# Other places in memory for the score tiles and the mask tiles, a VectorE add, unfilled gather tiles and another order of expert items

## The chip, the cores and the metric

One core of a Trainium2 chip runs the whole program. The metric is the time of one execution in microseconds (us); the kernel before has a median of 2927.58 us over 3 runs. Below, PE is TensorE, DVE is VectorE, ACT is ScalarE, POOL is GpSimd, and SP is the engine that issues most of the transfers.

## The reference

One decoder layer over T = 2048 tokens of D = 1024. The first half reads one projection of the normalised input and feeds three mixers: gated linear attention (GLA), attention over the 256 best keys of each query by an indexer score (DSA), and a complex diagonal state space (S5). The second half sends each token to 2 of 32 experts.

```
proj = h @ w_in                                  # 2616 columns, cut into GLA, DSA, indexer, S5 parts
score = einsum('bqh,bqhs->bqs', iwb, relu(iq . ik));  _, sel = top_k(score, 256)   # per block of 128 queries
p = softmax(q . k[sel]);  o_dsa = p @ v[sel]
x1 = x + gate1 * (concat([o_gla, o_dsa, o_s5]) @ w_out)
h2 = rms_norm(x1) * (1 + scale2) + shift2        # xn * g2r + s2r in the kernel
y  = sum over the 2 experts of  weight * (silu(h2 @ w_gate[e]) * (h2 @ w_up[e])) @ w_down[e]
out = rms_norm(x1 + gate2 * y)
```

## The kernel before, in words

Queries are worked in 16 blocks of 128. The parts that matter here follow each other.

**Scores** (to about 413 us). `ts`, `s1c` and `s1` are the pools of this stage. `s1c` and `s1` hold inputs and weights that are finished first, `ts` holds the rows `sb` in which the score of a block is summed on DVE (line 256) up to the end. Each block is stored to `score_d` (line 263).

**Sweeps, select and masks** (to about 756 us). Three pieces of one generator, `sweep2`, go over the tokens: token-major columns (32 rows `ot`, finished on DVE in line 209), the GLA queries and keys (no DVE finish, but DVE and POOL split their weights, line 467), and more token-major columns (16 rows `ot` of 128 elements for DVE). Their tiles lie in the pool `fp`. POOL issues the loads `xx` of the activations (line 440), SP those of the weights (`wstage`, line 175). Beside them runs `select`: the scores of blocks 2 to 15 come back into the tiles `scr` (line 509, 8.7 MB in all, pool `tks`), and ten iterations count the keys above a threshold, nine blocks on ACT (line 804), five on DVE (line 807), and move the threshold (lines 811 and on). `masks` then finds the exact threshold: per block the tile `pen` is written (line 857, DVE), the score is subtracted (line 858, POOL for blocks 2, 4, 6, 8, 10, else DVE), its eight largest are taken (line 859, DVE); some small operations follow (lines 865 to 882), and then for each block the mask `mk` is written (line 885) and stored. `pen` (two buffers) and `mk` are in the pool `pn`. `s5_tables(0)` is woven in (lines 931 to 959, DVE).

**A branch** on a check of the masks (tile `fi`) is read by all engines; GLA and S5, attention and output projection come behind it.

**Routing and experts** (from about 1580 us). In the output projection each block computes x1 (lines 1726, 1728) and xn, adds `s2r` and stores to `h2_d` (lines 1735 to 1737); `route` scatters token lists to `tab_d` (POOL, line 1440). A short chain of small operations on the counts of tokens then ranks the experts, and the loop takes 32 items in a fixed order, each with a fixed capacity from the list `CAP`, the expert of that rank being read at run time. Even items are the full ones, odd items the small ones. Each item gathers rows into the tiles `xg` and later `part` (POOL, lines 1877 and 2004, three buffers each, filled with zeros once in line 1832).

The program is written by a scheduler that fixes the order on each engine at build time from the waits it knows, memory among them: a tile may be written only when what lay in its place has been released, and the pools are placed as stacks on the two sides of memory.

Of the kernel before, what the change touches and what calls it, by code (L numbers as in the profile page):

```python
# [11 lines left out]
BF = mybir.dt.bfloat16  # L12
# [3 lines left out]
OP = mybir.AluOpType  # L16
# [4 lines left out]
P = 128  # L21
T = 2048
# [18 lines left out]
def body(tc, x, c, ada_w, ada_b, norm1_g, w_in, gla_gate_w, gla_gate_b, gla_norm_g, dsa_norm_g,  # L41
         s5_a_re, s5_a_im, s5_log_step, s5_b_re, s5_b_im, s5_c_re, s5_c_im, s5_d, s5_glu_w,
         s5_glu_b, s5_norm_g, w_out, norm2_g, router_grp_w, router_grp_b, router_exp_w,
         router_exp_b, exp_w_gate, exp_w_up, exp_w_down, final_norm_g, out, stop=None, dbg=None):
# [3 lines left out]
    V, S, G, TE = nc.vector, nc.scalar, nc.gpsimd, nc.tensor  # L48
# [175 lines left out]
    ssq = con.tile([P, NB], F32, name="ssq")  # L224

    p1x = ExitStack()
    ts_ = p1x.enter_context(tc.tile_pool(name="ts", bufs=1, side="right"))
    s1c = p1x.enter_context(tc.tile_pool(name="s1c", bufs=1, side="right"))
    s1 = p1x.enter_context(tc.tile_pool(name="s1", bufs=2, side="right"))
    s1p = p1x.enter_context(tc.tile_pool(name="s1p", bufs=1, space=PSUM, side="right"))  # L230
    pr = s1p.tile([P, 16], F32, name="pr", tag="pp", bufs=1, padded_shape=[P, C1])
    eps = ts_.tile([P, T], F32, name="eps")
# [177 lines left out]
    for ch in range(8):  # L410
        side = chain(tok1(ch), prep(ch + 1) if ch < 7 else ())
# [320 lines left out]
    NE, TW = 32, 8  # L732
    tab_d = dr.tile([NE * T, TW], F32, name="tab_d")
    h2_d = dr.tile([T + 1, D], F32, name="h2_d")
    yp_d = dr.tile([T + 1, D], F32, name="yp_d")
# [108 lines left out]
    def masks(blks, act, z, pn):  # L844
        lo, cl, cnt, up, dn, f, w = sels.pop(z)
        n_b, b0 = len(blks), blks[0]

        def tt(nm):
            return tk.tile([P, n_b], F32, name=nm, tag=f"tk{z}_{nm}", bufs=1)

        ntau, pv = tt("ntau"), tt("pv")
        tops = tk.tile([P, n_b, 8], F32, name=f"tops{z}")
        V.tensor_scalar(w, cl, -float(TOPK), None, op0=OP.add)
        for n, b in enumerate(blks):
            nk = (b + 1) * P
            pen = pn.tile([P, T], F32, name="pen")
            V.tensor_scalar(pen[:, :nk], scr[b], lo[:, n:n + 1], -4.0 * BIG, op0=OP.is_lt, op1=OP.mult)
            (G if b in GP else V).tensor_sub(pen[:, :nk], pen[:, :nk], scr[b])
            V.max(tops[:, n], pen[:, :nk])
            yield  # L860
        if act:

            wa, la = w[:, 0:act], lo[:, 0:act]
            for j, d in ((0, cnt), (1, dn)):
                V.scalar_tensor_tensor(d[:, 0:act], la, -1.0, tops[:, 0:act, j], op0=OP.mult, op1=OP.is_equal)
            V.scalar_tensor_tensor(wa, cnt[:, 0:act], 0.5, wa, op0=OP.mult, op1=OP.add)
        V.tensor_scalar(f, w, -1.0, None, op0=OP.add)
        for n, b in enumerate(blks):
            j8 = tk.tile([P, 8], F32, name="j8", bufs=2)
            V.scalar_tensor_tensor(j8, iota8, w[:, n:n + 1], tops[:, n], op0=OP.is_equal, op1=OP.mult,  # L870
                                   accum_out=ntau[:, n:n + 1])
            V.scalar_tensor_tensor(j8, iota8, f[:, n:n + 1], tops[:, n], op0=OP.is_equal, op1=OP.mult,
                                   accum_out=pv[:, n:n + 1])
        V.tensor_tensor(up, ntau, pv, op=OP.is_equal)
        V.scalar_tensor_tensor(up, w, 0.5, up, op0=OP.is_gt, op1=OP.mult)
        if act:
            V.tensor_max(up[:, 0:act], up[:, 0:act], dn[:, 0:act])
        fb_ = fail[:, b0:b0 + n_b]
        V.scalar_tensor_tensor(fb_, w, 7.5, up, op0=OP.is_gt, op1=OP.max)
        V.scalar_tensor_tensor(fb_, w, -0.5, fb_, op0=OP.is_lt, op1=OP.max)  # L880
        V.tensor_scalar(ntau, ntau, -1.0, None, op0=OP.mult)
        for n, b in enumerate(blks):
            nk = (b + 1) * P
            mk = pn.tile([P, T], BF, name="mk", bufs=2)
            V.tensor_scalar(mk[:, :nk], scr[b], ntau[:, n:n + 1], -BIG, op0=OP.is_lt, op1=OP.mult)
            nc.sync.dma_start(mask_d[b, :, :nk], mk[:, :nk])
            yield
# [4 lines left out]
    side = [chain(gates(), params(), empty_lists())]  # L892
# [3 lines left out]
    pn = pnx.enter_context(tc.tile_pool(name="pn", bufs=2, side="right"))  # L896
# [106 lines left out]
    with tc.tile_pool(name="fb", bufs=1) as fb, tc.tile_pool(name="fbp", bufs=1, space=PSUM) as fbp:  # L1003
# [8 lines left out]
        with tc.For_i(0, nf, 1):  # L1012
            for b in range(2, NB):
                nk = (b + 1) * P
                _, (fv,) = nc.values_load_multi_w_load_instructions(fi[0:1, b:b + 1], min_val=0, max_val=1)
                with tc.If(fv > 0):
# [9 lines left out]
                    mk = fb.tile([P, T], BF, name="mkf")  # L1026
# [421 lines left out]


    CAPR = [240] + [208] * 3 + [192] * 2 + [176] * 3 + [160] * 2 + [152, 148, 144, 140, 136, 132, 132] + [128] * 2 + [124] + [120] * 3 + [116, 112, 108, 104, 104, 100, 92, 88]  # L1450
    CAP = [CAPR[15 - p // 2] if p % 2 == 0 else CAPR[16 + p // 2] for p in range(NE)]
    capr = con2.tile([NE, NE], F32, name="capr")
    for o in range(2):
        for r in range(o, NE, 2):
            if r < 2 or CAP[r] != CAP[r - 2]:
                G.memset(capr[:, r::2], float(CAP[r]))

# [13 lines left out]
    with tc.tile_pool(name="da", bufs=2) as da, tc.tile_pool(name="dp", bufs=1, space=PSUM) as dp:  # L1471
# [44 lines left out]
        part = {}  # L1516
# [131 lines left out]
    with tc.tile_pool(name="a2c", bufs=1) as ac, tc.tile_pool(name="a2", bufs=2) as a2, \  # L1648
# [19 lines left out]
        gt1r, g2r, s2r = [ac.tile([P, D], F32, name=z) for z in ("gt1r", "g2r", "s2r")]  # L1668
# [45 lines left out]
        for b in range(NB):  # L1714
            nk = (b + 1) * P
            mh, ml, xb = nxt
            if b + 1 < NB:
                nxt = out_load(b + 1)
            x1 = a2.tile([P, D], F32, name="x1")
            tail = out_tail(*prev) if prev is not None else iter(())  # L1720
            for c in range(2):
                cs = slice(c * 512, (c + 1) * 512)
                pw = ap_.tile([P, 512], F32, name="pw", bufs=3)
                for k in range(KD):
                    mm3(pw, (mh[:, k], ml[:, k]), (wo[0][:, k, cs], wo[1][:, k, cs]), k, KD - 1)
                V.tensor_mul(x1[:, cs], pw, gt1r[:, cs])
                next(tail, None)
            V.tensor_add(x1, x1, xb)
            nc.sync.dma_start(yp_d[b * P:nk], x1)
            jk = a2.tile([P, D], BF, name="jk", bufs=1)  # L1730
            S.activation(jk, x1, AF.Square, accum_out=msq[:, b:b + 1])
            V.tensor_scalar(msq[:, b:b + 1], msq[:, b:b + 1], 1.0 / D, EPS, op0=OP.mult, op1=OP.add)
            rs = rsqrt_(a2, msq[:, b:b + 1], 1, "rsx")
            xn = a2.tile([P, D], F32, name="xn")
            V.scalar_tensor_tensor(xn, x1, rs, g2r, op0=OP.mult, op1=OP.mult)
            G.tensor_add(xn, xn, s2r)
            nc.sync.dma_start(h2_d[b * P:nk], xn)
            prev = (b, x1, rs)
        for _ in out_tail(*prev):
# [19 lines left out]
    with tc.tile_pool(name="rkp", bufs=1, space=PSUM) as rkp:  # L1759
# [9 lines left out]
        rc = rk.tile([NE, 2], F32, name="rc")  # L1769
# [5 lines left out]

        pf_ = rk.tile([NE, 2], F32, name="pf_")
        V.tensor_scalar(pf_[:, 0:1], rc[:, 0:1], 15.5, None, op0=OP.is_gt)
        V.tensor_scalar(pf_[:, 1:2], rc[:, 0:1], 4.0, -61.0, op0=OP.mult, op1=OP.add)
        V.tensor_mul(pf_[:, 0:1], pf_[:, 0:1], pf_[:, 1:2])
        V.tensor_scalar(rc[:, 0:1], rc[:, 0:1], -2.0, 30.0, op0=OP.mult, op1=OP.add)  # L1780
        V.tensor_add(rc[:, 0:1], rc[:, 0:1], pf_[:, 0:1])
        V.tensor_scalar(oh, iota32[0:NE], rc[:, 0:1], None, op0=OP.is_equal)
        V.scalar_tensor_tensor(tA, oh, 1.0, capr, op0=OP.mult, op1=OP.mult, accum_out=rc[:, 1:2])
# [42 lines left out]
    WRB, WHB = 11, 8  # L1826
    CM = max(CAP[0::2]), max(P, max(CAP[1::2]))

    xgt, partt = [[mx_.tile([P, D], F32, name=f"{z}{i}", bufs=1) for i in range(3)] for z in ("xg", "part")]
    sxt = [mx_.tile([P, 2], F32, name=f"sx{i}", bufs=1) for i in range(4)]  # L1830
    for t_ in xgt + partt:
        G.memset(t_, 0.0)
    for t_ in sxt:
        G.memset(t_, 1.0)

    def turn(tiles):
        tiles.append(tiles.pop(0))
        return tiles[-1]

    def load_list(pl, row, C):  # L1840

# [28 lines left out]
    def gather(C, pl, ix):  # L1870

        nb = 1 if C <= P else 2
        n = C // nb
        xgs = []
        for j in range(nb):
            xg = turn(xgt)
            G.indirect_dma_start(out=xg[:n], out_offset=None, in_=h2_d[:, :],
                                 in_offset=bass.IndirectOffsetOnAxis(ap=ix[:n, 0, j:j + 1], axis=0),
                                 bounds_check=T - 1, oob_is_err=False)
            xgs.append(xg)  # L1880
        return n, nb, pl, ix, xgs

# [115 lines left out]
    def partial(st):  # L1998

        n, nb, pl, ix, xgs = st  # L2000
        parts = []
        for j in range(nb):
            part = turn(partt)
            G.indirect_dma_start(out=part[:n], out_offset=None, in_=yp_d[:, :],  # L2004
                                 in_offset=bass.IndirectOffsetOnAxis(ap=ix[:n, 0, j:j + 1], axis=0),
                                 bounds_check=T - 1, oob_is_err=False)
            parts.append(part)
        return parts

# [106 lines left out]
    with tc.For_i(0, na, 1) as it:  # L2116
# [3 lines left out]
        with tc.If(fv > 0):  # L2120
# [9 lines left out]
            ix = lists(mo3, pl, 1, ky[:, :, None].to_broadcast([P, 1, 2]))  # L2130
# [39 lines left out]
```

## Time and profile before

| | us |
|---|---|
| median of 3 runs | 2927.58 (2925.64 to 2934.74) |
| the profiled execution | 2917.04 |
| its span, first to last instruction | 2914.7 |
| PE busy | 2391.7 (82%) |
| DVE busy | 2026.0 (70%) |
| ACT busy | 1288.2 (44%) |
| POOL busy | 800.7 (27%) |

The profiled execution is one execution, 10.5 us below the median of the others; it has 2.3 us outside its span. Shares are over the whole span; the stages differ much, so that a stage is read by its own stretch.

### The profile page before, as it was taken

To read this page: it belongs to the slowest core of one execution; us is meant where nothing else is said; L and a number is where in the kernel's file an instruction comes from. 1 tells how busy PE (TensorE), PEld (TensorE's weight loads), DVE (VectorE), ACT (ScalarE), POOL (GpSimd) and SP (SyncE) were. 2 spreads that over 40 slices of the span, in tenths; PEclk is the share of its full clock that TensorE was granted. 3 is DMA by queue.
4 is the path that set the end of the run, shared out by engine and by line. 5 is a ranking of instruction groups with operands and counts; after the bars stand their busy time and mean duration, and the time that the engine had idled before them with its cause. 6 is when DMAs were issued, how large, how long until landed. Compare 5 with 4: busy or idle time off the path is not lost. (4 is left out here: it accounts for less than half of the span.)

```text
span 2914.7 us, 38620 instructions
## 1 busy us (share of the span) xinstructions
PE 2391.7 (82%) x12563; PEld 1863.7 (64%) x12563; DVE 2026.0 (70%) x4838; ACT 1288.2 (44%) x2273; POOL 800.7 (27%) x733
## 2 busy tenths in 40 slices
PE   3989877798688899668997999487877889899995
PEld 3766645797566688556775887376555666566662
DVE  6568867898688745457885566677756677666764
ACT  2568866661122243356754222254433434444442
POOL 2221121324000111265543353323322322222221
PEclk9999967898677799778998999598989999999997
DMA  7333277989511565343314443677877878788872
GB/s 228 119 126 111 76 224 230 208 224 243 166 46 52 165 183 139 114 137 106 100 61 151 145 135 120 171 256 219 256 232 231 264 239 255 251 280 255 263 246 68
DMA packets 414518, 516.87 MB, mean 177 GB/s; under 512 B 87203, under 2 KB 314691, under 8 KB 414053
## 3 DMA queue, kind: packets, MB, share of 16 engines
q1 hardware_dynamic: 309157, 396.66, 42.7%
q0 software_dynamic: 105152, 117.68, 16.0%
q8 instruction: 100, 1.64, 0.2%
q14 instruction: 109, 0.89, 0.1%
HBM read 419.31 MB, written 120.62 MB: 185 GB/s over the span
## 5 line engine op out<-in xcount | busy, mean ns | idle before, releaser
L1920 DVE TENSOR_TENSOR wl<-wraw,wh 128x1024 fp32r<-128x1024 f32 x272 | 329.0, 1221 | 166.0 <-ACT wh L1919 156.6
L1919 ACT ACTIVATE wh<-wraw 128x1024 fp32r<-128x1024 f32 x272 | 286.1, 1054 | 311.9 <-PE pd L165 111.1
L1969 PE MATMUL pg<-xT,wh 128*128 128x352 f32 (+10 forms) x1152 | 327.8, 364 | 19.3 <-DVE xT L1901 13.0
L1943 PE MATMUL pg<-wraw,xT 128*120 128x512 f32 (+9 forms) x448 | 229.0, 672 | 79.4 <-DVE ga__22979 L1976 11.5
L1971 PE MATMUL pg<-xT,wl 128*128 128x176 f32 (+10 forms) x1152 | 284.6, 247 | 0.7 <-DVE wl L1920 0.7
L440 POOL DMA_DIRECT2D xx<-hx_d x128 | 98.0, 770 | 573.6 <-PE ptk L1141 242.5
L1969 PEld LDWEIGHTS pg<-xT,wh 128*128 128x128 f32 x1152 | 226.0, 196 | 24.5 <-DVE xT L1901 14.9
L1971 PEld LDWEIGHTS pg<-xT,wl 128*128 128x128 f32 x1152 | 229.1, 199 | 1.3 <-DVE wl L1920 1.0
L1943 PEld LDWEIGHTS pg<-wraw,xT 128*120 128x120 f32 (+9 forms) x448 | 86.9, 199 | 212.6 <-issue 118.3
L256 DVE SCALAR_TENSOR_TENSOR sb<-rl,iws,sb 128x1024 f32<-128x1024 f32 (+7 forms) x154 | 178.0, 1156 | 35.2 <-ACT rl L255 26.0
L163 PE MATMUL pd<-wh,hid 128*104 128x512 f32 (+17 forms) x400 | 163.5, 409 | 25.3 <-DVE y L1995 13.1
L2017 POOL DMA_INDIRECT yp_d<-y,ix x50 | 86.5, 1729 | 323.9 <-DVE y L2014 182.3
L255 ACT ACTIVATE rl<-pi,iwa 128x1024 f32<-128x1024 f32 (+7 forms) x176 | 157.4, 910 | 30.0 <-DVE sb L256 19.8
L163 PE MATMUL pp<-xx,w 128*128 128x256 f32 x512 | 152.5, 298 | 15.0 <-ACT w L466 7.2
L164 PE MATMUL pd<-wl,hid 128*104 128x512 f32 (+17 forms) x400 | 159.2, 398 | 0.0
L165 PE MATMUL pd<-wh,hid 128*104 128x512 f32 (+17 forms) x400 | 158.7, 402 | 0.0
L165 PE MATMUL pp<-xx,w 128*128 128x256 f32 x512 | 150.1, 294 | 5.5 <-DVE w L467 5.2
L164 PE MATMUL pp<-xx,w 128*128 128x256 f32 x512 | 149.0, 291 | 1.6 <-DMA xx<-hx_d 1.6
L252 PE MATMUL pi<-iks,iqs 128*128 128x512 f32 (+3 forms) x304 | 111.1, 449 | 28.1 <-ACT rl L255 27.3
L1537 DVE CUSTOM_DVE_ANT_0 pr<-ps,mk 128x512 f32<-128x512 f32 (+3 forms) x160 | 94.4, 605 | 50.1 <-PE ps L1536 29.3
L163 PE MATMUL pj<-w,xx 128*128 128x512 f32 (+1 forms) x256 | 98.8, 387 | 30.2 <-DVE ot L209 16.8
L2004 POOL DMA_INDIRECT part<-yp_d,ix x50 | 71.5, 1429 | 168.4 <-DMA yp_d<-y,ix 159.1
(1075 smaller groups left out, 6675.8 us busy)
## 6 DMA issues: line engine op xcount, KB each, us to landing
xx<-hx_d POOLq DMA_DIRECT2D x128, 512.0 KB
wraw<-in_exp_w_gate_dram SPq DMA_DIRECT2D x128, 512.0 KB
wraw<-in_exp_w_up_dram SPq DMA_DIRECT2D x128, 512.0 KB
wraw<-in_exp_w_down_dram SPq DMA_DIRECT2D x128, 512.0 KB
w<-in_ada_w_dram SPq DMA_DIRECT2D x64, 256.0 KB
w<-in_ada_w_dram SPq DMA_DIRECT2D x16, 512.0 KB
xi<-in_x_dram SPq DMA_DIRECT2D x16, 512.0 KB
hx_d<-xh SPq DMA_DIRECT2D x16, 512.0 KB
```

The lines of the kernel that those rows point to most:

```text
L163: TE.matmul(ps, st[0], mv[0], start=(k == first), stop=False, **kw)
L164: TE.matmul(ps, st[0], mv[1], start=False, stop=False, **kw)
L165: TE.matmul(ps, st[1], mv[0], start=False, stop=(k == last), **kw)
L252: TE.matmul(pi[:, s0:s0 + sl], iqs[:, h, i * P:(i + 1) * P], iks[:, g0 + s0:g0 + s0 + sl], start=True, stop=True)
L255: S.activation(rl[:, :gl], pi[:, :gl], AF.Relu, scale=iwa[:, b, h:h + 1])
L256: V.scalar_tensor_tensor(sb[:, gs], rl[:, :gl], iws[:, b, h:h + 1], (eps if h == 0 else sb)[:, gs], op0=OP.mult, op1=OP.add)
L440: G.dma_start(xx[j][-1], hx_d[j][k0:k0 + 4, :, t0:t0 + C1].rearrange("k p t -> p k t"))
L1919: S.activation(wh, w, AF.Copy)
L1920: V.tensor_sub(wl, w, wh.bitcast(F32))
L1943: TE.matmul(pgs[a][:C], xT[:, kk], wp[2 * i + a][:, k], start=(kk == 0), stop=(kk == KD - 1))
L1969: TE.matmul(pgs[m], wh[:, k, ws], xT[:, i * 4 + k], start=(i + k == 0), stop=False, skip_group_check=True)
L1971: TE.matmul(pgs[m][:, 0], wl[:, k, ws], xT[:, i * 4 + k, 0], start=False, stop=(i + k == 4), skip_group_check=True)
```

## The change

Five edits.

1. The pools of the score stage are opened in another order. Before, byte addresses per partition were `ts` 169952 to 229344, `s1c` 111584 to 169952, `s1` 40416 to 111584; now `s1c` 170976 to 229344, `s1` 99808 to 170976, `ts` 40416 to 99808. The tiles `scr` (161248 to 229344) and the sweep pool `fp` (34944 to 125056) stay where they were.
2. `mk` gets four buffers. The pool `pn` was 126560 to 151136 and becomes 118368 to 151136, whose low end lies below the high end of `fp`.
3. `xn + s2r` goes from POOL to DVE.
4. The six fills of `xg` and `part` go; each of these tiles is filled by a first gather of 128 rows with no bound check.
5. `CAP` for the even items starts at 140 and rises to 240 at item 28, and item 30 gets 136; before it rose from 136 to 240 at item 30. The rank arithmetic follows.

```diff
-    ts_ = p1x.enter_context(tc.tile_pool(name="ts", bufs=1, side="right"))
     s1c = p1x.enter_context(tc.tile_pool(name="s1c", bufs=1, side="right"))
     s1 = p1x.enter_context(tc.tile_pool(name="s1", bufs=2, side="right"))
+    ts_ = p1x.enter_context(tc.tile_pool(name="ts", bufs=1, side="right"))
...
-            mk = pn.tile([P, T], BF, name="mk", bufs=2)
+            mk = pn.tile([P, T], BF, name="mk", bufs=4)
...
-    CAP = [CAPR[15 - p // 2] if p % 2 == 0 else CAPR[16 + p // 2] for p in range(NE)]
+    CAP = [CAPR[(14 - p // 2) % 16] if p % 2 == 0 else CAPR[16 + p // 2] for p in range(NE)]
...
-            G.tensor_add(xn, xn, s2r)
+            V.tensor_add(xn, xn, s2r)
...
-        V.tensor_scalar(rc[:, 0:1], rc[:, 0:1], -2.0, 30.0, op0=OP.mult, op1=OP.add)
+        V.tensor_scalar(pf_[:, 1:2], rc[:, 0:1], 14.5, 32.0, op0=OP.is_gt, op1=OP.mult)
+        V.tensor_add(pf_[:, 0:1], pf_[:, 0:1], pf_[:, 1:2])
+        V.tensor_scalar(rc[:, 0:1], rc[:, 0:1], -2.0, 28.0, op0=OP.mult, op1=OP.add)
...
-    for t_ in xgt + partt:
-        G.memset(t_, 0.0)
     for t_ in sxt:
-        G.memset(t_, 1.0)
+        V.memset(t_, 1.0)
+    filled = set()
...
+    def rows(tile, src, ix, n):
+        if id(tile) in filled:
+            kw = dict(bounds_check=T - 1, oob_is_err=False)
+        else:
+            filled.add(id(tile))
+            n, kw = P, {}
+        G.indirect_dma_start(out=tile[:n], out_offset=None, in_=src[:, :],
+                             in_offset=bass.IndirectOffsetOnAxis(ap=ix[:n], axis=0), **kw)
```

**SP, around the return of the scores.** Before, the weights of the first sweep (`wstage`, in `fp`) and those of the second (`wz`) are issued ahead of the last two score stores, and all `scr` loads behind them:

```order
L175 DMA wstage<-in_w_in_dram 128x2x256 x8
L464 DMA wz<-in_w_in_dram 128x2x384 x2
L263 DMA score_d<-sb 128x1920
L263 DMA score_d<-sb 128x2048
L509 DMA scr_3418<-score_d 128x384
L509 DMA scr_3419<-score_d 128x512
L509 DMA scr_3420<-score_d 128x640
L509 DMA scr_3421<-score_d 128x768
```

Of the change, the stretch in which the loads stand (line numbers are one higher):

```order
L510 DMA scr_3427<-score_d 128x1536
L510 DMA scr_3428<-score_d 128x1664
L264 DMA score_d<-sb 128x1920
L510 DMA scr_3429<-score_d 128x1792
L510 DMA scr_3430<-score_d 128x1920
L525 DMA wg<-in_gla_gate_w_dram 16x4x48
L530 DMA gb_3738<-in_gla_gate_b_dram 48x1 x4
L539 DMA lr<-lr_d 16x1024
L264 DMA score_d<-sb 128x2048
L539 DMA lr<-lr_d 16x1024
L510 DMA scr_3431<-score_d 128x2048
L175 DMA wstage<-in_w_in_dram 128x2x256 x6
```

Thirteen of the fourteen `scr` loads have moved ahead of the last score store, and the weights of the first sweep stand behind the last `scr` load.

**DVE, at the end of select.** Before, the rows of `masks` begin right behind the last step of the threshold, and those of the third sweep (`w`, `ot`) stand among them, as here some twenty rows on:

```order
L857 TENSOR_SCALAR pen<-scr_3426,lo 128x1408
L178 TENSOR_TENSOR w_5492<-wstage,w_5491 128x2x384
L859 MAX tops_6524<-pen 128x8
L857 TENSOR_SCALAR pen<-scr_3427,lo 128x1536
L858 TENSOR_TENSOR pen<-pen,scr_3427 128x1536
L178 TENSOR_TENSOR w_5492<-wstage,w_5491 128x2x384
L859 MAX tops_6524<-pen 128x8
L209 SCALAR_TENSOR_TENSOR ot<-ot,pj 128x128
L859 MAX tops_6524<-pen 128x8
L209 SCALAR_TENSOR_TENSOR ot<-ot,pj 128x128
L857 TENSOR_SCALAR pen<-scr_3428,lo 128x1664
L857 TENSOR_SCALAR pen<-scr_3429,lo 128x1792
```

Of the change, from the end of select on:

```order
L854 TENSOR_SCALAR w<-cl 128x14
L178 TENSOR_TENSOR w_5492<-wstage,w_5491 128x2x384 x2
L209 SCALAR_TENSOR_TENSOR ot<-ot,pj 128x128 x16
L858 TENSOR_SCALAR pen<-scr_3418,lo 128x384
L858 TENSOR_SCALAR pen<-scr_3419,lo 128x512
L932 TENSOR_TENSOR va<-bb_3697,par 128x768
L860 MAX tops_6524<-pen 128x8
L859 TENSOR_TENSOR pen<-pen,scr_3419 128x512
L858 TENSOR_SCALAR pen<-scr_3420,lo 128x640
L860 MAX tops_6524<-pen 128x8
```

All sixteen rows `ot` of the third sweep now stand ahead of the first `pen`, and the table rows (`va`, `t4v`) stand among the mask rows. The first `pen` waits for the release of the pool `fp`.

**POOL, at the start of the expert loop.** Before, the last two scatters of token lists have fills among and behind them, and the first gathers, a little further on, take 68 rows each:

```order
L1832 MEMSET xg_18274 128x1024
L1440 DMA tab_d<-pay_18172,ix_18173 65536x8
L1832 MEMSET xg_18275 128x1024
L1440 DMA tab_d<-pay_18181,ix_18182 65536x8
L1832 MEMSET xg_18276 128x1024
L1832 MEMSET part_18277 128x1024
L1832 MEMSET part_18278 128x1024
L1832 MEMSET part_18279 128x1024
```

Of the change:

```order
L2052 MEMSET pl_18298 128x16
L1441 DMA tab_d<-pay_18172,ix_18173 65536x8
L1441 DMA tab_d<-pay_18181,ix_18182 65536x8
L1849 DMA xg_18276<-h_d,ix_18371 128x1024
L1849 DMA xg_18277<-h_d,ix_18371 128x1024
L1849 DMA xg_18278<-h_d,ix_18371 128x1024
L1849 DMA xg_18276<-h_d,ix_18371 66x1024
L1849 DMA part_18279<-yp_d,ix_18371 128x1024
```

The fills are gone, and the first gathers take 128 rows.

## Rows read from the trace of the kernel before

**Rows 1.** Busy time by stretch: PE, PEld, DVE, ACT, POOL, granted clock, DMA share, GB/s.
```profile
400.00:470.00 70.00, 48.91 (x157) 33.54 (x156) 39.38 (x76) 35.52 (x57) 6.83 (x10) 0.74 0.68 225
470.00:545.00 75.00, 62.98 (x256) 48.81 (x254) 59.68 (x155) 54.93 (x99) 16.93 (x23) 0.94 1.02 224
545.00:657.00 112.00, 98.40 (x773) 97.17 (x774) 106.01 (x340) 70.12 (x128) 34.97 (x41) 0.92 0.81 212
657.00:674.00 17.00, 4.76 (x19) 3.33 (x18) 16.89 (x13) 2.79 (x4) 11.63 (x8) 0.65 0.68 179
674.00:750.00 76.00, 70.17 (x375) 69.53 (x375) 52.70 (x127) 11.91 (x33) 24.92 (x46) 0.92 0.95 260
750.00:797.00 47.00, 26.55 (x88) 19.37 (x88) 30.15 (x83) 9.59 (x17) 0.00 (x0) 0.55 0.50 147
```

**Rows 2.** Timeline at the end of the scores: start, length, engine, line.
```profile
407.72 2.67 DVE L256 SCALAR_TENSOR_TENSOR sb<-rl,iws,sb 128x1024 f32<-128x1024 f32 x2
...
408.88 0.80 PE L163 MATMUL pj<-w,xx 128*128 128x512 f32 x1 [1.56 <-ACT rl L255]
...
418.15 13.22 SPq L509 DMA_DIRECT2D scr<-score_d  x14
...
439.54 1.81 DVE L807 TENSOR_SCALAR_CACHE_REDUCE j<-scr,t 128x1536 bf16<-128x1536 f32 x1 [0.65 <-DMA scr<-score_d]
```

**Rows 3.** Timeline of DVE: the step that closes select iterations 1, 7 and 10.
```profile
461.08 0.17 DVE L812 TENSOR_SCALAR up<-cnt 128x14 f32<-128x14 f32 x1
...
607.79 0.17 DVE L812 TENSOR_SCALAR up<-cnt 128x14 f32<-128x14 f32 x1
...
648.95 0.18 DVE L812 TENSOR_SCALAR up<-cnt 128x14 f32<-128x14 f32 x1
```

**Rows 4.** Timeline: the wait between sweeps 2 and 3, the last sweep row, the first table row.
```profile
674.06 0.84 ACT L177 ACTIVATE w<-wstage 128x768 fp32r<-128x768 f32 x1 [13.11 <-DMA wstage<-in_w_in_dram]
...
750.14 0.29 DVE L209 SCALAR_TENSOR_TENSOR ot<-ot,pj 128x128 f32<-128x128 f32 x1 [2.48 <-ACT ot L208]
756.64 0.96 DVE L931 TENSOR_TENSOR va<-bb,par 128x768 f32<-128x768 f32 x1 [4.06 <-DMA dv_d<-ot]
```

**Rows 5.** Groups of instructions, 640 to 760: count, busy us, mean ns, idle before.
```profile
L859 DVE MAX8 tops<-pen 128x8 f32<-128x384 f32 (+13 forms) x14 | 19.8, 1417 | 0.0
L858 DVE TENSOR_TENSOR pen<-pen,scr 128x512 f32<-128x512 f32 (+8 forms) x9 | 19.7, 2192 | 0.1
L857 DVE TENSOR_SCALAR pen<-scr,lo 128x384 f32<-128x384 f32 (+13 forms) x14 | 15.5, 1132 | 0.3 <-issue 0.2
L885 DVE TENSOR_SCALAR mk<-scr,ntau 128x384 bf16<-128x384 f32 (+13 forms) x14 | 11.8, 853 | 18.0 <-DMA mask_d<-mk 18.0
L858 POOL TENSOR_TENSOR pen<-pen,scr 128x384 f32<-128x384 f32 (+4 forms) x5 | 11.5, 2294 | 15.5 <-DVE pen L857 15.5
L870 DVE SCALAR_TENSOR_TENSOR j<-iota,w,tops 128x8 f32<-128x8 f32 x14 | 2.6, 226 | 0.0
```

**Rows 6.** Timeline at the start of the expert loop: POOL, then DVE.
```profile
1822.17 2.34 POOL L1736 TENSOR_TENSOR xn<-xn,s2r 128x1024 f32<-128x1024 f32 x1 [13.00 <-DVE pay L1436]
1837.82 2.75 POOL L1832 MEMSET part<- 128x1024 f32 x3
1852.25 1.21 POOL L1877 DMA_INDIRECT xg<-h_d,ix  x1 [11.50 <-issue]
...
1822.63 1.90 DVE L1387 TENSOR_TENSOR t<-lg,gm 128x4 f32<-128x4 f32 x1
...
1837.16 3.62 DVE L1806 COPY fj<-ce 32x16 f32<-32x16 f32 x1
```

**Rows 7.** Line 1728: shortest, median and longest ns, first and last start.
```profile
L1728 DVE TENSOR_TENSOR x<-x,xb x16: 1215/2414/2766, 1591.2 to 1811.9; 128x1024 f32<-128x1024 f32 x16
```

**Rows 8.** Busy time by stretch as in rows 1, and ACT, last expert pair.
```profile
2820.00:2840.00 20.00, 20.00 (x121) 17.47 (x120) 16.34 (x31) 9.39 (x16) 5.61 (x3) 1.00 0.64 189
...
2842.86 1.06 ACT L1919 ACTIVATE wh<-wraw 128x1024 fp32r<-128x1024 f32 x1 [6.82 <-DMA wraw<-in_exp_w_down_dram]
```

More of the change, by code (lines that the diff above doesn't have):

```diff
@@ L1777, in body @@
         V.tensor_scalar(pf_[:, 0:1], rc[:, 0:1], 15.5, None, op0=OP.is_gt)
-        V.tensor_scalar(pf_[:, 1:2], rc[:, 0:1], 4.0, -61.0, op0=OP.mult, op1=OP.add)
+        V.tensor_scalar(pf_[:, 1:2], rc[:, 0:1], 4.0, -91.0, op0=OP.mult, op1=OP.add)
         V.tensor_mul(pf_[:, 0:1], pf_[:, 0:1], pf_[:, 1:2])
-        V.tensor_scalar(rc[:, 0:1], rc[:, 0:1], -2.0, 30.0, op0=OP.mult, op1=OP.add)
+        V.tensor_scalar(pf_[:, 1:2], rc[:, 0:1], 14.5, 32.0, op0=OP.is_gt, op1=OP.mult)
+        V.tensor_add(pf_[:, 0:1], pf_[:, 0:1], pf_[:, 1:2])
+        V.tensor_scalar(rc[:, 0:1], rc[:, 0:1], -2.0, 28.0, op0=OP.mult, op1=OP.add)
         V.tensor_add(rc[:, 0:1], rc[:, 0:1], pf_[:, 0:1])
@@ L1876, in gather @@
             xg = turn(xgt)
-            G.indirect_dma_start(out=xg[:n], out_offset=None, in_=h2_d[:, :],
-                                 in_offset=bass.IndirectOffsetOnAxis(ap=ix[:n, 0, j:j + 1], axis=0),
-                                 bounds_check=T - 1, oob_is_err=False)
+            rows(xg, h2_d, ix[:, 0, j:j + 1], n)
             xgs.append(xg)
@@ L2003, in partial @@
             part = turn(partt)
-            G.indirect_dma_start(out=part[:n], out_offset=None, in_=yp_d[:, :],
-                                 in_offset=bass.IndirectOffsetOnAxis(ap=ix[:n, 0, j:j + 1], axis=0),
-                                 bounds_check=T - 1, oob_is_err=False)
+            rows(part, yp_d, ix[:, 0, j:j + 1], n)
             parts.append(part)
```

## The prediction

> **What bounds the kernel now.** I read the busy times by stretch first, to find which engine each piece of the program waits for, then the timeline of DVE where the change puts its hands, then the groups of instructions of the mask stage. The page says PE 82%, but that is a mean; four of the five edits lie between 400 and 800 us, where it is not so. In the stretch of the first sweep PE is busy 48.9 of 70 and 63.0 of 75 us, of the second 98.4 of 112, then there is a hole of 17 us with 4.8 of work, and the third sweep has 70.2 of 76 [rows 1]. So the sweeps do not run at PE's pace. DVE has hardly a gap from 545 to 674 (106.0 of 112 and 16.9 of 17), and is at 52.7 of 76 while the third sweep runs, with the masks among it. What ends the stage is the third sweep: its last row `ot` stands at 750.14, the first table row waits for its store until 756.64 [rows 4], and then comes table work with DVE at 30.2 of 47. The masks, 14 x 3 large rows on DVE, are over by then: they cost the path nothing today. That cover is what I look at.
>
> **Scores to select (edit 1).** Before, the last score rows on DVE run from 407.72 for 2.67 us, the 14 loads `scr` are issued from 418.15 on, over 13.2 us, and DVE's first count starts at 439.54, behind a load [rows 2]; the first of ten iterations closes at 461.08, the tenth at 648.95. Undisturbed, an iteration takes (648.95 - 607.79) / 3 = 13.7 us [rows 3]. Now 13 of the 14 tiles are in memory before the scores end, and only the last has its round trip through `score_d` still ahead. I let iteration 1 run from 418 to 432: 29 us sooner. The other nine took 187.9 us, of which 9 x 13.7 = 123 are their own and 65 are sweep rows, parameter rows and waits. If that sum stays, select ends at 620; I take 625, since the sweep it has to serve on the way begins later.
>
> **The price of it.** The sweep pool now lies over `ts`, which holds the score rows to the end. The activation loads on POOL and the weight loads on SP must wait for it, and the latter stand behind the last `scr` load. Before, PE starts the sweep at 408.88, waiting only for the scores [rows 2]. Now some 4 MB (by their shapes four tiles `xx` of 512 KB, eight `wstage` of 256 KB) must come first from about 413, at the 225 to 260 GB/s of the neighbouring stretches [rows 1]: 16 to 18 us, so a start at about 431, 22 us late. Of this little is lost at once: PE stood a third of the time up to 470 in any case.
>
> **When do the sweeps end?** Busy time times granted clock gives what they need at full rate: sweep 1 about 91 us (48.9 x 0.74 less 4 for scores, plus 63.0 x 0.94), sweep 2 98.4 x 0.92 = 90.5 and 3 in the hole, sweep 3 70.2 x 0.92 = 64.6 [rows 1]. With no wait at all, 431 + 91 + 93 + 65 plus some 8 each for new weights gives 696: the early bound. But on DVE the rows of sweep 1 stand in the order through iteration 6, and the second half of the weights of sweep 2 in iteration 7. Iteration 6 closes at 432 + 5 x 13.7 = 500 plus most of the 65, that is at about 545, so sweep 2 has its weights at 545 to 555 and ends 92 us later, near 643. The hole behind it was a wait of 13.11 us for a weight load [rows 4], whose buffer POOL freed late, behind its subtractions for the masks; these go to the back, so the hole shrinks from 17 to about 7. Sweep 3 then takes 70 to 72: **X, its end, is 722**, 28 us sooner. The late bound is 750: nothing won.
>
> **The masks (edit 2).** With four buffers the pool of `pen` and `mk` reaches into the sweep pool, and the first `pen` waits until that is released. The order shows it: sixteen rows `ot`, then the first `pen`. So the masks, which ran beside sweep 3, come behind it, with the tables between them, all on DVE and ahead of the branch that every engine reads. Queued behind are GLA, S5 and all later stages. Their length is from [rows 5]: 19.8 + 19.7 + 15.5 + 11.8 = 66.8, and two lots of 14 small rows of 0.226 make 6.3; rows that follow each other overlap by about a tenth of a us, so I take 70. POOL's five subtractions (11.5) run beside. From this go about 7: the table rows fill some gaps of DVE in 750 to 797 (17 us idle [rows 1], most of it the release wait and the branch, which stay). **E, the masks laid bare, is 63.** From below 53 (all 17 filled), from above 72 (nothing filled, and waits on POOL's rows). What the four buffers save is the 18.0 us in which `mk` waited for stores [rows 5]: these ended ahead of 750 and cost nothing; with the masks laid bare, two buffers would cost up to that much more.
> The Trainium skill (Perfetto Trace Analysis, Optimization Strategy) says that where the most loaded engine changes from regime to regime, interleaving the regimes can help. This change takes one such interleaving apart; rows 1 show both engines at work in 674 to 750 before. By that rule alone the whole 70 would be lost; what it leaves out is the earlier end of the sweeps.
>
> **The add on DVE (edit 3).** Sixteen rows more on DVE; the nearest, line 1728, takes 1.22 us alone. But its median is 2.41 [rows 7]: it stands beside POOL's add of 2.34 us [rows 6] and waits for it. So DVE pays 16 x 1.2 and gets back about 16 x 1.2: 0, with bounds of -3 and +3, and PE has its own work over it. On the last block nothing covers it: there the small row of line 1387 took 1.90 us, and the scatters stood behind the add [rows 6]; about -1.7.
> The Trainium skill (GPSIMD Engine Reference, Specifications) has POOL share its memory interface with DVE, in contention with DVE rows of two inputs from SBUF. The trace agrees (1.22 against 2.41); without the rule the add would be charged 19.5 us of DVE time, hidden under PE.
>
> **Fills and first gathers (edit 4).** The fills of `part` hold POOL for 2.75 us, and a small DVE row on the chain to the expert list takes 3.62 beside them [rows 6]; without them about 0.2: -3.3. The first gathers fetch 128 rows in place of 68; one row of POOL is 1.21 us [rows 6], the landing may grow by up to 1.5. Edits 3 and 4 at the loop's start together: **-4**, between -6 and 0.
>
> **Order of items (edit 5).** The last pair is the lighter for 104 fewer rows. PE is full in 2820 to 2840, but ACT then waits 6.82 us for weights of the same pair [rows 8], so that less PE work uncovers transfers. I take **-4**, between -8 and +2, and 0 for the same rows put into the pair before, which transfers cover.
>
> **The sum** on the profiled execution: -28 + 63 - 4 - 4 = +27, so 2917.0 + 27 = 2944. The median of the runs is 10.5 above the profiled execution; I add that: **2954**.
>
> **The rivals.**
> - *Faster.* The sweeps run nearly without waits, X = 697, and the masks cost E = 53: the stage gives 0, start and tail -5 and -8: 2917 - 13 + 10.5 = 2915. It decides from X + E below 749. For it: DVE is nearly empty after select, and the transfers of the sweeps had pauses. Against: the weights of sweep 2 stand in DVE's order behind six iterations. 0.12.
> - *No change.* X = 705, E = 60: +15 - 8 = +7, 2934. 0.10.
> - *The sweeps win nothing.* Started 22 us late and bound to DVE's order, sweep 1 and 2 end where they did, X = 750: +63 - 8 = +55, 2983. For it: sweep 2 in the order hangs on iteration 7, and DVE was 95% busy there. 0.18.
> - *The order of items does nothing*, because the loop hangs on transfers: +31, 2958, within the forecast.
>
> My forecast, X from 712 to 740 with E near 63, has 0.60. About 0.3% (9 us) is what a measurement can tell from no change. That makes slower 0.78, same 0.10, faster 0.12. The range: 2925 keeps out most of the faster case, 2988 takes in X = 750 with E a little higher; together they leave out about 2 in 10. The likeliest case alone is 2940 to 2975.
>
> **What would show it.** Right: first count on DVE near 420, first matmul of the sweep near 431, tenth iteration closed near 625, last `ot` near 722, then 14 `pen` and `mk` with PE nearly idle for some 65 us, hardly a wait on mask stores, the branch some 35 later than before; gathers of the first item 4 sooner against the routing. Wrong: a first `pen` that starts before the last `ot`; sweeps that end below 695; masks of less than 55 us.

## The result and the profile after

The changed kernel has a median of 2968.43 us (2965.82 to 2972.24, 4 runs) against 2926.61 for the kernel before beside it; the ratio is 1.0139, 95% interval 1.0116 to 1.0162: slower by 1.4%, some 41 us (34 to 47). The prediction was 2954, within 2925 to 2988.

The stretches of [rows 1] in the changed kernel, with the same columns:

```profile
400.00:470.00 70.00, 45.74 (x162) 32.71 (x163) 56.57 (x109) 52.98 (x87) 20.77 (x23) 0.73 0.87 240
470.00:545.00 75.00, 61.73 (x250) 47.64 (x249) 57.54 (x154) 53.84 (x100) 16.63 (x21) 0.92 0.93 213
545.00:657.00 112.00, 98.92 (x776) 97.74 (x776) 76.57 (x297) 53.31 (x97) 32.50 (x42) 0.91 0.81 214
657.00:674.00 17.00, 14.12 (x69) 13.15 (x68) 3.00 (x4) 5.04 (x9) 7.15 (x7) 0.90 0.82 214
674.00:750.00 76.00, 57.17 (x325) 55.86 (x323) 21.03 (x35) 11.78 (x31) 20.96 (x23) 0.88 0.82 207
750.00:797.00 47.00, 5.38 (x22) 4.07 (x21) 42.55 (x84) 2.52 (x4) 7.16 (x2) 0.50 0.03 8
```

DVE's load has moved. In 545 to 657 it falls from 106.0 to 76.6 of 112, in 674 to 750 from 52.7 to 21.0 of 76; in 750 to 797 it rises from 30.2 to 42.6 of 47, while PE has 5.4 of work and the transfers stand still (a share of 0.03). That is the signature of work that lost its cover: one engine full, the others waiting.

The timeline of the changed kernel at the places of [rows 2 to 4] (start, length, engine, line; lines behind 226 are one higher):

```profile
434.10 0.79 PE L163 MATMUL pj<-w,xx 128*128 128x512 f32 x1 [9.41 <-DMA xx<-hx_d]
...
432.54 0.17 DVE L813 TENSOR_SCALAR up<-cnt 128x14 f32<-128x14 f32 x1
...
623.43 0.18 DVE L813 TENSOR_SCALAR up<-cnt 128x14 f32<-128x14 f32 x1
...
729.21 0.29 DVE L209 SCALAR_TENSOR_TENSOR ot<-ot,pj 128x128 f32<-128x128 f32 x1 [1.80 <-ACT ot L208]
731.91 0.82 DVE L858 TENSOR_SCALAR pen<-scr,lo 128x384 f32<-128x384 f32 x2 [2.41 <-DMA dv_d<-ot]
732.64 1.75 DVE L932 TENSOR_TENSOR va<-bb,par 128x768 f32<-128x768 f32 x1
...
822.83 0.17 DVE L1011 CAST fi<-fl 128x17 int32<-128x17 f32 x1
```

PE has the first two matmuls of the sweep at 423.47 and goes on at 434.10, behind a load; before, the sweep starts at 408.88. The first select iteration closes at 432.54 and the tenth at 623.43, before at 461.08 and 648.95. The last row `ot` is at 729.21, before at 750.14; right behind it stands the first `pen`, having waited for the release of the sweep pool. The check `fi`, which every engine reads at the branch, is made at 822.83; before it was at 774.54. So the stage ends 48.3 us later: its sweeps 20.9 sooner, the way from there to `fi` 93.6 in place of 24.4, which is 69.2 longer. DVE, third of the busy times, fills that way (the changed kernel, then the kernel before):

```profile
729.21:822.83 93.62, 12.21 (x46) 9.49 (x46) 85.59 (x189) 6.55 (x10) 14.78 (x26) 0.51 0.27 87
...
750.14:774.54 24.40, 9.07 (x36) 7.06 (x36) 14.75 (x47) 6.16 (x10) 0.00 (x0) 0.59 0.71 218
```

Each of these is the time of one execution. The control below, the same program as the kernel before, has its last `ot` at 747.54 and `fi` at 770.03, and the five other runs that leave this stage as it was have 745.55 to 749.98 and 769.11 to 773.76: differences of less than 5 us between two traces are not told from chance here.

The groups of the mask stage, as in [rows 5], from 725 to 830:

```profile
L860 DVE MAX8 tops<-pen 128x8 f32<-128x384 f32 (+13 forms) x14 | 19.9, 1421 | 5.5 <-POOL pen L859 5.5
L859 DVE TENSOR_TENSOR pen<-pen,scr 128x512 f32<-128x512 f32 (+8 forms) x9 | 14.4, 1597 | 0.0
L859 POOL TENSOR_TENSOR pen<-pen,scr 128x384 f32<-128x384 f32 (+4 forms) x5 | 13.3, 2664 | 35.3 <-DVE pen L858 35.3
L886 DVE TENSOR_SCALAR mk<-scr,ntau 128x384 bf16<-128x384 f32 (+13 forms) x14 | 11.8, 847 | 0.1
L858 DVE TENSOR_SCALAR pen<-scr,lo 128x384 f32<-128x384 f32 (+13 forms) x14 | 11.6, 845 | 2.4 <-DMA dv_d<-ot 2.4
```

The 18.0 us of waits of `mk` for its stores are gone (0.1 is left), and the large rows are cheaper than they were beside the sweep: the subtractions 14.4 for 19.7, `pen` 11.6 for 15.5. The waits were hidden before, so that their end wins nothing. The cheaper rows do count, since they lie bare: 57.7 us for the four groups on DVE, 66.8 before.

At the start of the expert loop, POOL and then PE, as in [rows 6]:

```profile
1884.43 0.97 POOL L1441 DMA_INDIRECT tab_d<-pay,ix  x1 [0.30 <-DVE tA L1773]
1900.03 1.00 POOL L1849 DMA_INDIRECT xg<-h_d,ix  x1 [14.63 <-issue]
...
1904.55 1.17 PE L1906 MATMUL pt<-ident,xg 70*128 70x70 f32 x8 [15.93 <-DMA xg<-h_d,ix]
```

From the last scatter to the first gather 15.6 us pass (16.3 from 1835.95 to 1852.25 before), from the first gather to the first transpose 4.5; before it was 8.0 (1852.25 to 1860.29). From the last row of line 1728 to that transpose it is 42.4 us in place of 48.4.

### The profile page after: what moved, and what is told of

It reads as the page before. It is cut to its first block, busy times and chain, and to the rows that moved or that the text cites. A ratio compares the mean times of both kernels' runs of the same rounds, so it can differ in the third digit from the quotient of the medians.

```text
span 2967.0 us, 38585 instructions
## 1 busy us (share of the span) xinstructions
PE 2385.9 (80%) x12563; PEld 1856.6 (63%) x12563; DVE 2025.2 (68%) x4860; ACT 1287.7 (43%) x2273; POOL 766.7 (26%) x707
## 3 DMA queue, kind: packets, MB, share of 16 engines
q0 software_dynamic: 105408, 119.28, 15.6%
## 5 line engine op out<-in xcount | busy, mean ns | idle before, releaser
L257 DVE SCALAR_TENSOR_TENSOR sb<-rl,iws,sb 128x1024 f32<-128x1024 f32 (+7 forms) x154 | 175.7, 1141 | 34.1 <-ACT rl L256 24.7
L253 PE MATMUL pi<-iks,iqs 128*128 128x512 f32 (+3 forms) x304 | 113.2, 455 | 20.9 <-ACT rl L256 19.4
```

The costliest lines, as they stand in the source:

```text
L253: TE.matmul(pi[:, s0:s0 + sl], iqs[:, h, i * P:(i + 1) * P], iks[:, g0 + s0:g0 + s0 + sl], start=True, stop=True)
L257: V.scalar_tensor_tensor(sb[:, gs], rl[:, :gl], iws[:, b, h:h + 1], (eps if h == 0 else sb)[:, gs], op0=OP.mult, op1=OP.add)
```

## The experiments

Each ratio is to the kernel before, timed beside it on the same chip.

**Edit 1 alone.**

```diff
-    ts_ = p1x.enter_context(tc.tile_pool(name="ts", bufs=1, side="right"))
     s1c = ...
     s1 = ...
+    ts_ = p1x.enter_context(tc.tile_pool(name="ts", bufs=1, side="right"))
```

> Edit 1 alone (the kernel before with the score pools in the new order; two mask buffers, so that the mask pool stays clear of the sweep pool). Theory A, that edit 1 ends the sweeps some 21 us sooner (729 in the changed kernel against 750) and that only the bare masks of edit 2 make the loss: about 2906, select closed near 624, last sweep row near 727, masks among the third sweep. Theory B, that the later start of the sweeps is itself the loss: 2927 or more.

Measured: ratio 1.0020 (0.9994 to 1.0046). Neither theory: no gain, and no clear loss. Its timeline on DVE:

```profile
622.32 0.17 DVE L812 TENSOR_SCALAR up<-cnt 128x14 f32<-128x14 f32 x1
...
697.21 1.08 DVE L885 TENSOR_SCALAR mk<-scr,ntau 128x640 bf16<-128x640 f32 x2 [3.98 <-DMA mask_d<-mk]
708.63 0.82 DVE L885 TENSOR_SCALAR mk<-scr,ntau 128x1152 bf16<-128x1152 f32 x1 [4.04 <-DMA mask_d<-mk]
746.84 0.69 DVE L1080 SCALAR_TENSOR_TENSOR gq<-gq,eb 128x512 f32<-128x512 f32 x1 [8.34 <-ACT eb L1077]
756.52 0.29 DVE L209 SCALAR_TENSOR_TENSOR ot<-ot,pj 128x128 f32<-128x128 f32 x1 [1.79 <-ACT ot L208]
```

Select is done at 622.32, 27 us sooner than before, as foreseen. But the last `ot` is at 756.52, 6 us later. The masks also begin sooner, `mk` waits for stores 20.5 us in all (here 3.98 and 4.04 at a time) with rows `ot` of the third sweep behind it on DVE, and towards the end a GLA row that waits 8.34 us for ACT stands ahead of the last four `ot`. PE is at 7.8 of 12 us in 700 to 712. PE's second sweep ends at 654.96, 3.2 sooner than before, and from the start of the third to the last `ot` it is 100.7 us, before 91.1. So most of the time won in select is gone when the third sweep starts, and the rest is waited away in it; which of these waits holds it is read from one timeline and not shown.

**Edit 2 alone.**

```diff
-            mk = pn.tile([P, T], BF, name="mk", bufs=2)
+            mk = pn.tile([P, T], BF, name="mk", bufs=4)
```

> Edit 2 alone (four mask buffers, the mask pool reaching into the sweep pool). Theory A: all 14 pen rows stand behind the last sweep row, 69 us of masks and tables more behind it, less some 10 because the hole ahead of the third sweep shrinks: about 2985. Theory B, that the masks cost little where they stand: 2927 to 2935. A third view, that four buffers help by the 18 us of waits on stores: about 2910.

Measured: ratio 1.0193 (1.0168 to 1.0217), some 56 us. Timeline and groups:

```profile
732.41 0.29 DVE L209 SCALAR_TENSOR_TENSOR ot<-ot,pj 128x128 f32<-128x128 f32 x1 [1.80 <-ACT ot L208]
735.10 0.82 DVE L857 TENSOR_SCALAR pen<-scr,lo 128x384 f32<-128x384 f32 x2 [2.40 <-DMA dv_d<-ot]
...
825.84 0.17 DVE L1010 CAST fi<-fl 128x17 int32<-128x17 f32 x1
...
L859 DVE MAX8 tops<-pen 128x8 f32<-128x384 f32 (+13 forms) x14 | 19.9, 1419 | 5.5 <-POOL pen L858 5.5
L885 DVE TENSOR_SCALAR mk<-scr,ntau 128x384 bf16<-128x384 f32 (+13 forms) x14 | 11.7, 843 | 0.0
```

The last `ot` is at 732.41, 17.7 sooner than before, without edit 1. `fi` follows 93.4 later; the stage ends 51.3 later, though `mk` waits for no store any more (0.0). From the start of the third sweep on PE (659.20, before 659.04) to the last `ot` it is 73.2 us, before 91.1: without the masks that sweep runs 18 us shorter. Theory A stands; the view that ending the waits on stores is a gain falls for this place of the pool.

**All edits but the second.**

```diff
-            mk = pn.tile([P, T], BF, name="mk", bufs=4)   # the changed kernel
+            mk = pn.tile([P, T], BF, name="mk", bufs=2)
```

> The changed kernel with two mask buffers in place of four, all other edits kept. Theory A: the changed kernel's 2968 less the 69 us of bare masks, plus what the masks now take from the third sweep: 2900 to 2912. Theory B: about 2968, as the buffers would not matter.

Measured: ratio 1.0014 (1.0001 to 1.0027). The loss is gone (`fi` at 775.75), which is theory A's main point, but the further gain that it had for edit 1 is missing: the last `ot` is at 753.34. This run is edit 1 with edits 3 to 5, and its ratio is that of edit 1 alone (1.0020) within the intervals.

**Edit 5 alone** (the list `CAP` and its rank arithmetic, as in the change).

> Edit 5 alone (the other order of the even expert items). By the prediction: 4 us less from a lighter last pair, 2923. By the trace of the changed kernel, in which the distance to the kernel before grows by about 11 us from the first transposes of the loop to the last pair but one and then shrinks by 4: about 2934. If the order does nothing: 2927.

Measured: ratio 0.9995 (0.9976 to 1.0015), 7 us less to 4 more: no change is seen. The 7 more read out of the one trace fall; the 4 less of the prediction lie within the interval and are neither shown nor excluded. Its first gathers take 70 rows (POOL, then PE):

```profile
1855.56 1.04 POOL L1879 DMA_INDIRECT xg<-h_d,ix  x1 [11.51 <-issue]
...
1859.87 1.17 PE L1898 MATMUL pt<-ident,xg 70*128 70x70 f32 x8 [15.22 <-DMA pl<-tab_d]
```

4.3 us pass, not 8.0. Whether these 4 us are lost again in the loop the time does not tell: from the first transpose to the end it is 1052.2 us here, 1054.4 in the kernel before and 1060.3 in the control, the same program.

**Four mask buffers clear of the sweep pool**, on the changed kernel.

```diff
-            pen = pn.tile([P, T], F32, name="pen")
+            pen = pn.tile([P, T], F32, name="pen", bufs=1)
```

> The changed kernel with its four mask buffers, but one buffer for pen, so that the mask pool ends at 126560 again and stays clear of the sweep pool. Theory A (the loss is the overlap in memory, not the number of mask buffers): 2918 or a little below. If the third sweep is held by rows ot that stand on DVE behind mask rows waiting for a store (as in the run with edit 1 alone), four buffers take that wait away: last sweep row near 735 to 740, 2900 to 2910. Rival (four buffers cost as such): 2955 or more.

Measured: ratio 0.9968 (0.9951 to 0.9984). The rival falls: four buffers cost nothing as such, the overlap does (the one buffer for `pen` is part of this run). But the last `ot` is not at 735 to 740:

```profile
741.67 0.69 DVE L1081 SCALAR_TENSOR_TENSOR gq<-gq,eb 128x512 f32<-128x512 f32 x1 [6.80 <-ACT eb L1078]
751.47 0.29 DVE L209 SCALAR_TENSOR_TENSOR ot<-ot,pj 128x128 f32<-128x128 f32 x1 [1.79 <-ACT ot L208]
774.46 0.17 DVE L1011 CAST fi<-fl 128x17 int32<-128x17 f32 x1
```

Two GLA rows ahead of the last `ot` wait for ACT (6.80 and 2.05), as with edit 1 alone. The waits of `mk` for stores are 11.1 us here, 20.5 with edit 1 alone, and the third sweep takes 96.0 us to its last `ot`, 100.7 there. By these two traces they held it in part; the seven runs that leave this stage as it was need 88.6 to 91.1.

**The same on the kernel before**, with no other edit (`mk` four buffers, `pen` one).

> The kernel before with four mask buffers and one pen buffer, the pool clear of the sweep pool; no other edit. If the 18 us of waits on mask stores were hidden, as the prediction says: 2918, no change. If they held the third sweep through the rows ot behind them: 2903 to 2912.

Measured: ratio 0.9970 (0.9950 to 0.9989), 3 to 15 us less. Groups and timeline:

```profile
L885 DVE TENSOR_SCALAR mk<-scr,ntau 128x384 bf16<-128x384 f32 (+13 forms) x14 | 11.6, 853 | 6.2 <-DMA mask_d<-mk 6.0
L858 DVE TENSOR_TENSOR pen<-pen,scr 128x512 f32<-128x512 f32 (+8 forms) x9 | 14.4, 1605 | 0.1
...
747.79 0.29 DVE L209 SCALAR_TENSOR_TENSOR ot<-ot,pj 128x128 f32<-128x128 f32 x1 [1.80 <-ACT ot L208]
750.81 0.96 DVE L931 TENSOR_TENSOR va<-bb,par 128x768 f32<-128x768 f32 x1 [2.73 <-DMA dv_d<-ot]
762.50 0.17 DVE L1010 CAST fi<-fl 128x17 int32<-128x17 f32 x1
```

The waits on stores fall from 18.0 to 6.2, and the one `pen` buffer brings 11.6 us of waits for POOL's subtractions, which were 0.0. The last `ot` is 2.4 sooner than in the kernel before, but no sooner than in the control (747.54), so lengths tell more. From PE's start of the third sweep to the last `ot` it is 87.1 us, where the seven runs that leave this stage as it was have 88.6 to 91.1. To `fi` it is 101.8, there 112.5 to 115.5; some of this is only that `fi` now stands ahead of a row that waits for PE (3.05 us here). To the last row of line 1728 it is 1149.8, there 1152.7 to 1159.9, which fits the measured 3 to 15. So the waits were not wholly hidden, as the prediction had it. What in this run gives the gain, the shorter queue of mask stores or something else, was not tried by itself.

**Edit 3 alone.**

```diff
-            G.tensor_add(xn, xn, s2r)
+            V.tensor_add(xn, xn, s2r)
```

> Edit 3 alone (xn + s2r on VectorE). By the prediction 0 over the output projection and about -2 at its end: 2916. If the sixteen rows cost DVE time that PE waits for: up to 2935. The row of line 1728 should fall to 1.22 us throughout.

Measured: ratio 0.9983 (0.9966 to 1.0000). The output projection as in rows 1, and line 1728:

```profile
1580.00:1810.00 230.00, 222.17 (x1125) 185.36 (x1126) 156.25 (x486) 53.01 (x85) 66.48 (x41) 0.98 0.42 144
...
L1728 DVE TENSOR_TENSOR x<-x,xb x16: 1211/1874/2756, 1594.7 to 1815.2; 128x1024 f32<-128x1024 f32 x16
```

DVE has 156.3 of 230 us, 138.3 before; PE 222.2, 222.5 before. The 18 us on DVE are hidden, but they are not given back: line 1728 falls from 2.41 to 1.87 at its median, not to 1.22. The rows say why. In the kernel before, most of the slow rows of line 1728 stand beside another instruction of POOL, the subtraction of line 1660:

```profile
1695.46 2.40 POOL L1660 TENSOR_TENSOR ml<-mf,mh 128x1024 fp32r<-128x1024 f32 x1 [0.48 <-ACT mh L1659]
...
1696.39 2.55 DVE L1728 TENSOR_TENSOR x<-x,xb 128x1024 f32<-128x1024 f32 x1
```

Of the sixteen rows, eight lie beside that subtraction alone (2.53 to 2.77 us), three beside the add (2.29 to 2.30, two of them beside both) and five beside neither (1.22). With edit 3 the three fall to 1.21 or 1.22, and the eight stay at 2.53 to 2.76. Nor is anything won at the end of the projection: from the last row of line 1728 to the last scatter it is 24.7 us, before 24.1.

**Edit 4 alone** (no fills, first gathers of 128 rows), timed twice.

> Edit 4 alone (no fills, first gathers of 128 rows). By the prediction -3.3 from the list's small row and up to +1.5 from longer gathers: about 2916. By the trace of the changed kernel, where first gather to first transposes takes 4.6 us against 8.0: 2911 to 2914, and the gain is in the gathers, not in the fills.

> Edit 4 alone a second time, since 14 us less were measured where the trace shows about 6 (2 in the chain to the list, 3.5 in the gathers): -6 if the first timing was partly chance, -14 if it was not.

Measured: ratios 0.9938 (0.9913 to 0.9962) and 0.9963 (0.9940 to 0.9986); what lies in both intervals, 0.9940 to 0.9962, is 11 to 18 us. First gather and first transpose:

```profile
1855.66 1.00 POOL L1846 DMA_INDIRECT xg<-h_d,ix  x1 [15.13 <-DVE q__18373 L1867]
...
1860.20 1.14 PE L1903 MATMUL pt<-ident,xg 68*128 68x68 f32 x8 [17.27 <-DMA pl<-tab_d]
```

4.5 us in place of 8.0. From the last scatter to the list it is 3.7 (1839.56 to 1843.26) in place of 5.7, but the gather is issued 16.1 behind the scatter, before 16.3, so that these 2 us do not reach it. From the last row of line 1728 to the first transpose it is 43.7 us (42.7 in the second timing) in place of 48.4: the traces show 5 to 6; the rest of the gain stays open.

**The fills kept, the first gathers of 128 rows.**

```diff
+    for t_ in xgt + partt:
+        G.memset(t_, 0.0)
```

> The kernel before with the six fills kept on POOL, and the first gathers of each tile taking 128 rows. If the first gathers are what edit 4 gains by (8.0 to 8.8 us from first gather to first transpose wherever they take 68 rows, 4.3 with 70, 4.5 with 128): about 4.5 us in the trace, and 4 to 5 us less than the kernel before. If the gain is in the fills: 8 us in the trace, no change in time.

Measured: ratio 0.9967 (0.9949 to 0.9985). Fills, first gather, first transpose:

```profile
1840.09 2.75 POOL L1835 MEMSET part<- 128x1024 f32 x3
1854.46 1.01 POOL L1848 DMA_INDIRECT xg<-h_d,ix  x1 [11.57 <-issue]
...
1858.89 1.14 PE L1905 MATMUL pt<-ident,xg 68*128 68x68 f32 x8 [15.40 <-DMA pl<-tab_d]
```

With all the fills in place, the gather still takes 4.4, and the time, 4 to 15 us less, is that of edit 4 within the intervals. From the last row of line 1728 to the first transpose it is 44.8 us, 3.7 less than before, of the 5 to 6 that edit 4 shows there. So what the traces show of the gain is for the most part in the gathers. It is not the whole account: edit 5 alone has the same 3.7 (44.7 us) and no gain that can be measured.

**A control**, the kernel before under another name.

> The kernel before once more under a name of its own, beside the other runs of this call: what two timings of one program can differ by. 0, within 0.2%.

Measured: ratio 0.9993 (0.9976 to 1.0009). Its trace gives the play of a single execution: last `ot` 747.54 and `fi` 770.03, where the kernel before has 750.14 and 774.54.

**What the runs point to**: edits 3 and 4, and four mask buffers clear of the sweep pool; edits 1 and 5 left out.

> Edits 3 and 4, and four mask buffers beside one pen buffer, clear of the sweep pool; pools of the scores and order of items as before. By the single runs: -9 from the masks, -5 to -14 from edits 3 and 4: 14 to 23 us less than the kernel before.

Measured: ratio 0.9929 (0.9900 to 0.9958), median 2900.31 us against 2919.75: faster than both kernels.

```profile
740.25 0.29 DVE L209 SCALAR_TENSOR_TENSOR ot<-ot,pj 128x128 f32<-128x128 f32 x1 [1.80 <-ACT ot L208]
754.96 0.17 DVE L1010 CAST fi<-fl 128x17 int32<-128x17 f32 x1
```

The last `ot` is 9.9 sooner than in the kernel before (7.3 against the control) and `fi` is at 754.96, 19.6 sooner (15.1); the first gather to the first transpose takes 4.6 us. The last row of line 1728 is then only 6.3 sooner (3.8 against the control), so that the time of `fi` overstates what the masks give.

## Why the prediction was right, point by point

**The masks laid bare (E): right, 69 in place of 63, and in part by luck.** Edit 2 alone gives 69.0, the whole change 69.2. The change takes the interleaving of DVE's masks with PE's sweep apart, and that is the whole of the loss: without edit 2 the ratio is 1.0014, with four buffers clear of the sweep pool 0.9968. The parts were less good than the sum. The rows that I summed to 66.8 take 57.7 when no sweep runs beside them. I took 70 for all mask rows, where my own terms give 65 (66.8 and 6.3, less a tenth for each of 79 rows). The 7 us that I let table rows fill did not come; on the contrary, 16.9 us of the rows of lines 954 to 959 (one higher in the changed kernel) now stand ahead of `fi`, before 3.9, and POOL's subtractions add waits of 5.5. The errors made up for each other.

**The end of the sweeps (X): 729.2 for 722, right in sign and wrong in its cause.** I put 28 us down to edit 1, with 10 of them from the shorter hole. Edit 2 alone gives 17.7, and the 3.2 more that it has in company with edit 1 are within the play of single traces: what ends the sweeps sooner is above all that the third one is rid of mask rows, on DVE and on POOL. That part was foreseen for the hole: ACT's wait for the weights of the third sweep is 6.01 us in the changed kernel and 6.76 with edit 2 alone, before 13.11. The step that failed is "sweep 2 has its weights at 545 to 555 and ends 92 us later, near 643". The first split of these weights on DVE came in time, and the third sweep starts where it did (two rows of the changed kernel, two of the kernel before):

```profile
551.26 0.94 DVE L468 TENSOR_TENSOR w<-wz,w 128x768 fp32r<-128x768 f32 x1
656.69 0.80 PE L163 MATMUL pj<-w,xx 128*128 128x384 f32 x3 [0.87 <-ACT w L177]
...
554.39 0.94 DVE L467 TENSOR_TENSOR w<-wz,w 128x768 fp32r<-128x768 f32 x1
659.04 0.62 PE L163 MATMUL pj<-w,xx 128*128 128x384 f32 x2 [0.88 <-ACT w L177]
```

From that split to its last matmul (655.82, before 658.17) sweep 2 takes 104.6 us, before 103.8, and not 92: the 92 was busy time cut down to the full clock, while PE is busy 100.9 us from the first to the last matmul of sweep 2, at a granted clock of 0.90, and waits besides, 1.52 us ahead of the second split at 561.20 (561.52 before) and 4.45 for a row of ACT. So the second sweep, which I had ending 15 us sooner than before, ends 2.4 sooner. Sweep 3 took 73.4 us from there to the last `ot` where I had 79, which hides a part of it. A first sweep that starts 15 to 25 us later and catches up gains nothing for the second. That is half of the rival "the sweeps win nothing", and with edit 1 alone that rival is the truth.

**The select iterations: right** (432.5 and 623.4 for 432 and 625), and worth nothing by themselves.

**The waits on mask stores: I had them at nothing, and they cost some.** Clear of the overlap, four `mk` buffers with one for `pen` give 3 to 15 us; that it is the waits on stores that give them is not shown.

**The add: right in the sum (0), wrong in the reason.** I read the 2.41 us of line 1728 as a wait for POOL's add. It stood beside the add in three of sixteen rows and beside POOL's subtraction of line 1660 in eight, and those eight stay slow. So DVE does not get the time back, PE covers it; and the 1.7 us at the end of the projection do not come with edit 3 alone.

**Fills and gathers: -4 for some -6 in the traces, and wrong in place.** I charged the larger gathers up to +1.5, which no run shows; they are 3.5 to 3.6 shorter, and of the fills 1 to 2 us are left at the first transpose. Timed alone, edit 4 gives 11 to 18 us, outside my 0 to 6; what gives the rest is open.

**The order of items: -4 is not shown.** The ratio of edit 5 alone allows it and 0 as well. One trace alone would have misled.

The sum was +27, measured some +41. By the traces 7 of the difference is X and 6 is E; 4 more are the order of items if it does nothing, and 2 go off at the start of the loop. Each of these has a play of a few us, so the split is rough.

## What to carry to other kernels

A buffer count is also an address: before adding a buffer, see what the pool will then lie over, and when that is released; here 6.7 KB of each partition made the masks wait for the whole sweep pool. Ask of each stretch which of two engines is idle beside the other; here work under such a cover was free, and taking the cover away cost its whole length. And an engine that finishes early wins nothing as long as a row in another's fixed order still stands behind a wait: look for the last row on which the next stage hangs, and compare that row's time in both kernels, and in a second trace of one of them, since two executions of the same program differed by 2.6 us there.

## What the runs showed of the hardware that I had not expected

A gather of fewer rows can take longer. From the issue of the first gather to the first transpose of its rows, 68 rows took 8.0 to 8.8 us in six runs (8.04 in the kernel before, 8.76 with edit 3 alone, 8.50 in the control), 70 rows 4.3 in one (edit 5 alone), and 128 rows, of which 68 or 70 are then used, 4.4 to 4.6 in seven. The bytes do not explain it, nor does the bound check, which edit 5 alone keeps.
The Trainium skill (DMA: Bandwidth & Descriptors, Why a DMA increments its semaphore by 16 and not by 1) says that a transfer is spread over the largest number of engines, up to 16, that divides the slowest dimension of both its sides. Worked out from that rule, as an estimate, 68 rows would go over 4 engines, 70 over 14 and 128 over 16. The runs agree with that order, and so do the packets of 4 KB in the traces: in the first microsecond in which there are any, at most 5 or 6 were under way at once in the six runs with 68 rows, 15 with 70 rows and 16 to 19 with 128. These are counts of packets; the traces do not name the engine of each.
A row on DVE can be slow beside more than one instruction of POOL. The 128x1024 add of line 1728 took 1.22 us with no arithmetic on POOL beside it, 2.29 beside POOL's add and 2.53 to 2.77 beside POOL's subtraction of 2.40 us; taking the add away left the eight rows beside the subtraction as slow as they were.
